# Hybrid conv/mLSTM layer: the first value projection by feature tiles between the modulation rows, in a written order; output-weight splits one step later; two up-projection slots loaded early

## The chip, the cores and the metric

One core of one Trainium2 chip. The metric is device microseconds of one execution, the median of the runs. TensorE (PE) does the matmuls, VectorE (DVE), ScalarE (ACT) and GpSimd (POOL) the elementwise work, SyncE (SP) issues the transfers.

## The reference, cut to what matters

A layer over 128 context and 2048 latent tokens, model width 1024, in float32. Each token's modulation comes from one of two conditioning vectors:

```python
mod = silu(c) @ w_mod + b_mod              # shift1, scale1, gate1, shift2, scale2, gate2
h = rmsnorm(x, norm1) * (1 + scale1) + shift1
z = h @ w_in                               # conv parts, q, k, v, o, gates
h_m, C, n, m = mlstm_bidir(q, k, v, gates, C0, n0, m0)
x = x + gate1 * (concat([y_sc, h_m]) @ w_out)
h2 = rmsnorm(x, norm2) * (1 + scale2) + shift2
up = conv3(h2 @ w_up);  a, gg = split(up)
x = x + gate2 * ((silu(gg) * a) @ w_down)
```

## The kernel before

The 2176 tokens are 17 chunks of 128, in blocks of three chunks (384 tokens; block 5 has 256). Features lie on the partitions, in eight tiles of 128. A float32 operand is split into a rounded high and a low part (`wh`, `wl` for weights, `hH`, `hL` for activations), and a product is three matmuls: high by high, high by low, low by high.

The **start stage** has four parts. `mod_pe` (L617 to L622) computes one row of 128 modulation values: it loads 512 KB of `w_mod` into one of five `wm` buffers, runs eight matmuls into an accumulator bank and adds the bias on DVE into `modT`. `mods` calls it for the scale and the shift row of a feature tile, and `affine` (L138) makes the factor `ab` of that tile. Sixteen such rows are computed on PE, and the rest later on DVE by `mod_dve` (L663 to L665). `squares` (L180 to L184) sums the squares of a block of x, ACT squaring and DVE adding; `inv_rms` (L147 to L151) turns the sum into a root on PE, DVE and POOL; `apply` first spreads that root over the partitions (`spread`, L158), then makes the eight tiles of `hH` and `hL` (L196 to L206). Even tiles go DVE L196, ACT L200, DVE L201; odd tiles go DVE L196, ACT L204, ACT L205, POOL L206. `vg` (L389 to L396) is the value and gate projection: for each chunk and each half of the columns an accumulator takes 24 matmuls of 264 columns over all eight tiles, ACT copies the values out (`row`), DVE adds the gate bias. `vg` runs for block 3, with `prep(4)` (squares, root and `apply` of block 4) between its groups, for block 4 with `prep(5)`, then for block 5; `heads` (L224 to L226, with the copy out at L404) follows with k, q and o, and beside it runs `side`: `first_stats` (squares of blocks 0 to 2), `mod_dve` and `down_sums`.

`out_proj` (L547 to L610) is 48 steps of 24 matmuls into one accumulator. In each step DVE adds the result to the row of x (L600), which frees the accumulator, and ACT and DVE gather the squares (L566, L572). Weights come in pairs, two steps of each four load them and the other two split them; from step 21 on DVE makes `wl` (L130) in front of that step's L600.

In the first **up stage** a slot of seven needs a block `F`, written by `sums` to DRAM (`tD`) and read back (L304), and split on ACT (L314) and DVE (L315). `split` does both at one place.

The framework's scheduler sets each engine's order from priorities, except where `in_order` ties the instructions of each engine to the order of the program.

Of the kernel before, what the change touches and what calls it, by code (L numbers as in the profile page):

```python
# [42 lines left out]
def bc(ap, shape):  # L43
    return ap.to_broadcast(shape)
# [13 lines left out]
def hymba_kernel(ctx: ExitStack, tc: tile.TileContext, I, O):  # L58
# [63 lines left out]
    def load_w(src, n=1024):  # L122
        return split_w(get_w(src, n), n)

    def split_w(st, n=1024, whole=False):
        wh = wp.tile([P, WN], F32R, name="wh")
        S.activation(wh[:, :n], st[:, :n], AF.Copy)  # L127
        wl = wp.tile([P, WN], F32R, name="wl")
        if whole:
            V.tensor_sub(wl[:, :n], st[:, :n], wh[:, :n].bitcast(F32))  # L130
            return wh, wl
        for a in (0, n // 2):
            G.tensor_sub(wl[:, a:a + n // 2], st[:, a:a + n // 2], wh[:, a:a + n // 2].bitcast(F32))  # L133
        return wh, wl
# [35 lines left out]
    def rcol(b):  # L170
        t0, n = BL[b]
        return rc[:, t0 // P:(t0 + n) // P]
# [11 lines left out]
            V.tensor_add(ss[:, :n], ss[:, :n], sq[:, :n])  # L184
        return ss

    def apply(b, xt, norm):
        t0, n = BL[b]
        rb = spread(rcol(b), n)
        hH, hL = h_pair()  # L190
        sh = 0 if norm == 0 else 24
        for k in range(KT):
            x = xt[k // 4][:, k % 4]
            for a, e, v in spans(t0, t0 + n):
                a, e = a - t0, e - t0
                V.scalar_tensor_tensor(x[:, a:e], x[:, a:e], ab[:, norm, k, v:v + 1], rb[:, a:e],  # L196
                                       op0=ALU.mult, op1=ALU.mult)
                sv = modT[:, sh + k, v:v + 1]
                if k % 2 == 0:
                    S.activation(hH[:, k, a:e], x[:, a:e], AF.Identity, bias=sv)  # L200
                    V.scalar_tensor_tensor(hL[:, k, a:e], x[:, a:e], sv, hH[:, k, a:e].bitcast(F32),  # L201
                                           op0=ALU.add, op1=ALU.subtract)
                else:
                    S.activation(x[:, a:e], x[:, a:e], AF.Identity, bias=sv)  # L204
                    S.activation(hH[:, k, a:e], x[:, a:e], AF.Copy)  # L205
                    G.tensor_sub(hL[:, k, a:e], x[:, a:e], hH[:, k, a:e].bitcast(F32))  # L206
        return hH, hL
# [146 lines left out]
    with ExitStack() as ph1:  # L354
# [21 lines left out]
        def load_vg(j):  # L376
            return [load_w(I["w_vg"][j, kk], WN) for kk in range(2)]

        def vg(blocks, hs, ws):
            for b in blocks:  # L380
                hH, hL = hs[b]
                for j in range(2):
                    for c in chunks(b):
                        o = c * P - BL[b][0]
                        acc = acc_tile()
                        for k in range(KT):
                            w_h, w_l = (x[:, (k % 4) * 264:(k % 4 + 1) * 264] for x in ws[2 * j + k // 4])
                            a_h, a_l = hH[:, k, o:o + P], hL[:, k, o:o + P]
                            PE.matmul(acc[:, :264], a_h, w_h, start=(k == 0), stop=False)  # L389
                            PE.matmul(acc[:, :264], a_h, w_l, start=False, stop=False)  # L390
                            PE.matmul(acc[:, :264], a_l, w_h, start=False, stop=(k == KT - 1))
                        r = rp.tile([P, 384], F32, name="row")[:, :258].rearrange("p (h d) -> p h d", h=2)
                        G.memset(r[:, :, 128:129], 1.0)
                        S.activation(r[:, :, :P], acc[:, :256].rearrange("p (h d) -> p h d", h=2), AF.Copy)
                        Q.dma_start(vD[c][:, 2 * j:2 * j + 2], r)
                        V.tensor_add(gates[:, c, j * 8:(j + 1) * 8], acc[:, 256:264],  # L396
                                     bgate[:, j * 8:(j + 1) * 8])
                        yield

        def head(w, b, h, hs, dst, func, scale):  # L400
# [144 lines left out]
        def out_proj(grps, defer, ws, hook):  # L545
# [25 lines left out]
                if m:  # L571
                    V.tensor_add(sss[b][:, :n], sss[b][:, :n], sq[:, :n])  # L572

            rows, got, behind, squared, held, sss = [], [], [], [], [], {}
            for k in range(2):
                load_r(k)
            yield
            for k, (g, m, b) in enumerate(steps):
                grp, (t0, n) = grps[g], BL[b]
                hook()  # L580
                load_r(k + 2)
                while squared:
                    add(*squared.pop())
                if len(behind) > 1:
                    squared.append(close(*behind.pop(0)))
                if k + 4 < len(steps):
                    if k % 4 < 2:
                        got.append(get_w(I["w_out"][steps[k - k % 4 + 4 + k % 4][1]]))
                    else:
                        ws.append(split_w(got.pop(0), whole=k > 20))  # L590
                w, xr = ws[m % 2], rows.pop(0)
                acc = gemm(w, early[b], n)
                if k % 4 == 3:
                    del ws[:2]
                if held and k == held[0] + 4:
                    stats(held[1], [sss[b] for b in held[1]])
                    held = []
                for a, e, v in spans(t0, t0 + n):
# [13 lines left out]

        hs = {}
        with tc.tile_pool(name="start", bufs=1, side="right") as stp:
            def mod_pe(mt):
                st = stp.tile([P, 1024], F32, name="wm", bufs=5)
                Q.dma_start(st, I["w_mod"][mt])  # L617
                ps = acc_tile()
                for k in range(KT):
                    PE.matmul(ps[:, :P], st[:, k * P:(k + 1) * P], bc(csil[:, k, None, :], [P, 64, 2]),  # L620
                              start=(k == 0), stop=(k == KT - 1))
                V.tensor_scalar(modT[:, mt, :], ps[:, :2], bmod[:, mt:mt + 1], None, op0=ALU.add)  # L622

            def mods(k0, k1):
                for k in range(k0, k1):
                    mod_pe(8 + k)
                    mod_pe(k)
                    affine(0, k, k + 1)

            Q.dma_start(bmod, I["b_mod"])  # L630
            mod_pe(8)
            Q.dma_start(nrm, I["norms"])
            mod_pe(0)
            affine(0, 0, 1)
            Q.dma_start(ident, I["ident"])
            mods(1, 2)
            xs = {3: load_x(3, I["x"], xp, "xt", 2)}
            ss = squares(3, xs[3])
            mods(2, 4)
            ws = load_vg(0)  # L640
            inv_rms(ss, 384, rcol(3))
            mods(4, 8)
            hs[3] = apply(3, xs[3], 0)
            ws += load_vg(1)
            Q.dma_start(bgate, I["b_gate"].to_broadcast([P, 16]))
            cB = stp.tile([P, 2, 1024], F32, name="cB")

            def late():
# [18 lines left out]
                        affine(1, 0, KT)  # L667
                    yield

            def prep(b):  # L670
                xs[b] = load_x(b, I["x"], stp, "xs", 4)
                ss = squares(b, xs[b])
                yield
                inv_rms(ss, BL[b][1], rcol(b))
                yield
                hs[b] = apply(b, xs[b], 0)
                yield
# [42 lines left out]
            late()  # L720
            mod = mod_dve()
            side = chain(first_stats(mod), mod, down_sums())
            run(vg((3,), hs, ws), prep(4))
            run(vg((4,), hs, ws), prep(5))
            run(vg((5,), hs, ws))
            run(heads(BB, hs, 16, kD, AF.Copy, 1.0), side)
            run(heads(BB, hs, 12, qD, AF.Copy, QS), side)
# [392 lines left out]
        until(46, sums(0, fpool, (1,), (6, 0)))  # L1120
        prods = stages(st)
        ahead = [next(prods) for _ in range(2)]
        run(fill)
        in_order(first)

# [22 lines left out]
    with ph2:  # L1148
# [31 lines left out]
            V.tensor_mul(t2[:, 0, :n], t2[:, 0, :n], t2[:, 1, :n])  # L1180
            Q.dma_start(uD[j][:, hf * n:(hf + 1) * n], t2[:, 0, :n])

        split(0, ORDER[2])
        side = sums(1, fpool)
        cv = iter(())
        while ahead:
# [16 lines left out]
            if hf and j == FT - 1 and i == 0:  # L1203
                first_forms()
            if not hf and j == 0 and i + 3 < 7:
                split(0, ORDER[i + 3])
            kind = "ababaca"[i]
            for p in range(npair):
                if i in (0, 1, 5):
# [269 lines left out]
```

## Time and profile before

| | us |
|---|---|
| median of 3 runs | 2503.4 (2498.62 to 2506.39) |
| the profiled execution | 2510.81 |
| its span, first to last instruction | 2509.0 |
| PE busy | 2457.2 |
| DVE busy | 1637.3 |
| ACT busy | 1126.0 |
| POOL busy | 523.7 |

A row of the timeline gives the start in the span, the duration, engine, line and operation, and in brackets the idle time of that engine just before it with what ended it. PEclk is the granted TensorE clock, 1.00 being 2.4 GHz and 0.50 being 1.2 GHz.

### The profile page before, as it was taken

To read this page: it belongs to the slowest core of one execution; us is meant where nothing else is said; L and a number is where in the kernel's file an instruction comes from. 1 tells how busy PE (TensorE), PEld (TensorE's weight loads), DVE (VectorE), ACT (ScalarE), POOL (GpSimd) and SP (SyncE) were. 2 spreads that over 40 slices of the span, in tenths; PEclk is the share of its full clock that TensorE was granted. 3 is DMA by queue.
4 is the path that set the end of the run, shared out by engine and by line. 5 is a ranking of instruction groups with operands and counts; after the bars stand their busy time and mean duration, and the time that the engine had idled before them with its cause. 6 is when DMAs were issued, how large, how long until landed. Compare 5 with 4: busy or idle time off the path is not lost.

```text
span 2509.0 us, 42463 instructions
## 1 busy us (share of the span) xinstructions
PE 2457.2 (98%) x16127; PEld 2355.5 (94%) x16127; DVE 1637.3 (65%) x2670; ACT 1126.0 (45%) x2062; POOL 523.7 (21%) x468
## 2 busy tenths in 40 slices
PE   7999999999999999999999999999999999999998
PEld 7999999999999999989999999788888899999998
DVE  3994552332465676687678667876777786787586
ACT  3521153233545564364455445554555553444342
POOL 2442233121344450012112111022112200000000
PEclk9999999999999999999999999999999999999999
DMA  7873773365767887754125222522222286866674
GB/s 271 269 238 128 278 249 126 101 196 172 243 200 233 280 262 241 247 206 148 67 83 184 84 83 92 169 93 95 89 85 88 87 257 200 260 205 215 185 231 128
DMA packets 280766, 443.41 MB, mean 177 GB/s; under 512 B 23266, under 2 KB 206194, under 8 KB 278898
## 3 DMA queue, kind: packets, MB, share of 16 engines
q1 hardware_dynamic: 280562, 440.70, 53.8%
q8 instruction: 127, 2.08, 0.3%
q14 instruction: 77, 0.63, 0.1%
HBM read 334.72 MB, written 105.89 MB: 176 GB/s over the span
## 4 chain that ended last, share of the span: by engine, by line
PE 82%; DVE 7%; DMA 6%; ACT 2%; issue 2%; POOL 1%; SPq 0%; DVEq 0%; ACTq 0%; POOLq 0%
PE acc L224 9%; PE acc L226 9%; PE acc L225 9%; PE pa L1216 6%; PE pa L1218 6%; PE pa L1217 6%; PE d L1371 5%; PE d L1372 5%; PE d L1370 5%; PE pb L1216 3%; PE pb L1218 3%; PE pb L1217 3%; PE pc L1216 2%; PE pc L1217 2%; PE pc L1218 2%
## 5 line engine op out<-in xcount | busy, mean ns | idle before, releaser
L224 PE MATMUL acc<-hH,wh 128*128 128x384 f32 (+1 forms) x1536 | 511.9, 333 | 7.3 <-DVE row L600 5.5
L226 PE MATMUL acc<-hH,wl 128*128 128x384 f32 (+1 forms) x1536 | 504.9, 329 | 0.0
L225 PE MATMUL acc<-hL,wh 128*128 128x384 f32 (+1 forms) x1536 | 504.4, 328 | 0.0
L1370 PE MATMUL d<-bh,wh 128*128 128x272 f32 x1232 | 356.4, 290 | 0.7 <-ACT raw L1228 0.7
L1372 PE MATMUL d<-bh,wl 128*128 128x272 f32 x1232 | 356.8, 290 | 0.0
L1371 PE MATMUL d<-bl,wh 128*128 128x272 f32 x1232 | 356.1, 289 | 0.0
L1216 PE MATMUL pa<-tH,wh 128*128 128x288 f32 (+1 forms) x1056 | 348.1, 330 | 5.4 <-ACT tH L314 2.2
L1218 PE MATMUL pa<-tH,wl 128*128 128x288 f32 (+1 forms) x1056 | 347.5, 329 | 1.6 <-DVE wl L333 1.6
L1217 PE MATMUL pa<-tL,wh 128*128 128x288 f32 (+1 forms) x1056 | 347.8, 329 | 1.1 <-DVE tL L315 1.1
L333 POOL TENSOR_TENSOR wl<-st,wh 128x512 fp32r<-128x512 f32 x123 | 170.2, 1384 | 706.0 <-ACT wh L332 704.7
L224 PEld LDWEIGHTS acc<-hH,wh 128*128 128x128 f32 x1536 | 290.6, 189 | 8.8 <-issue 6.8
L133 POOL TENSOR_TENSOR wl<-wst,wh 128x512 fp32r<-128x512 f32 (+1 forms) x136 | 200.1, 1493 | 451.2 <-ACT wh L127 393.6
L225 PEld LDWEIGHTS acc<-hL,wh 128*128 128x128 f32 x1536 | 290.7, 189 | 0.3 <-issue 0.2
L226 PEld LDWEIGHTS acc<-hH,wl 128*128 128x128 f32 x1536 | 290.3, 189 | 0.2 <-issue 0.2
L1159 DVE SCALAR_TENSOR_TENSOR tt<-raw,fw,tt 128x127 f32<-128x127 f32 (+4 forms) x264 | 244.1, 945 | 1.4 <-ACT tt L1165 0.3
L1370 PEld LDWEIGHTS d<-bh,wh 128*128 128x128 f32 x1232 | 232.7, 189 | 1.3 <-ACT raw L1228 1.1
L1371 PEld LDWEIGHTS d<-bl,wh 128*128 128x128 f32 x1232 | 232.6, 189 | 0.2
L1372 PEld LDWEIGHTS d<-bh,wl 128*128 128x128 f32 x1232 | 232.5, 189 | 0.0
L1216 PEld LDWEIGHTS pa<-tH,wh 128*128 128x128 f32 x1056 | 198.9, 188 | 22.2 <-ACT wh L332 4.1
L1218 PEld LDWEIGHTS pa<-tH,wl 128*128 128x128 f32 x1056 | 199.7, 189 | 17.6 <-DVE wl L333 2.0
L1217 PEld LDWEIGHTS pa<-tL,wh 128*128 128x128 f32 x1056 | 199.3, 189 | 17.2 <-DVE tL L315 1.5
L332 ACT ACTIVATE wh<-s 128x512 fp32r<-128x512 f32 x176 | 110.8, 629 | 179.2 <-PE pc L1217 92.5
(250 smaller groups left out, 4829.3 us busy)
## 6 DMA issues: line engine op xcount, KB each, us to landing
st<-in_w_up SPq DMA_DIRECT2D x88, 512.0 KB, 4.5
us<-uD SPq DMA_DIRECT2D x48, 544.0 KB, 5.0
wst<-in_w_in SPq DMA_DIRECT2D x48, 512.0 KB, 3.7
uD<-tt SPq DMA_DIRECT2D x44, 544.0 KB, 2.7
R<-nD SPq DMA_DIRECT2D x34, 512.0 KB, 4.3
wm<-in_w_modr SPq DMA_DIRECT2D x32, 512.0 KB, 5.5
wst<-in_w_out SPq DMA_DIRECT2D x24, 512.0 KB, 5.0
st<-wsD SPq DMA_DIRECT2D x32, 384.0 KB, 3.1
```

Of the source, the lines that this page charges most:

```text
L133: G.tensor_sub(wl[:, a:a + n // 2], st[:, a:a + n // 2], wh[:, a:a + n // 2].bitcast(F32))
L224: PE.matmul(acc[:, :n], w_h, hH[:, k, :n], start=(k == 0), stop=False)
L225: PE.matmul(acc[:, :n], w_h, hL[:, k, :n], start=False, stop=False)
L226: PE.matmul(acc[:, :n], w_l, hH[:, k, :n], start=False, stop=(k == KT - 1))
L333: (G if on_pool else V).tensor_sub(wl, a, wh.bitcast(F32))
L1159: V.scalar_tensor_tensor(o, i, w, o, op0=ALU.mult, op1=ALU.add)
L1216: PE.matmul(acc, wh[:, w], rh, start=(kk == 0 and i in (0, 1, 5)), stop=False, skip_group_check=True)
L1217: PE.matmul(acc, wh[:, w], rl, start=False, stop=False, skip_group_check=True)
L1218: PE.matmul(acc, wl[:, w], rh, start=False, stop=(kk == 3), skip_group_check=True)
L1370: PE.matmul(acc, wh[:, c], uh, start=(kk == 0), stop=False)
L1371: PE.matmul(acc, wh[:, c], ul, start=False, stop=False)
L1372: PE.matmul(acc, wl[:, c], uh, start=False, stop=(kk == KH - 1))
```

## The change

**Start.** The two modulation rows of a feature tile share one `S` bank, of which there is one. The loads of x for block 3 are issued ahead of the third modulation row. The value projection of block 3 is done by feature tile: `vg_first(k)` adds tile k to all six groups (four accumulators and the two halves of `y`), eighteen matmuls, between the modulation rows or behind them. ACT copies the spread root of block 3 out of PSUM (`rb`); `norm` applies one or two tiles at a time. The squares, root and `norm` of block 4 and the squares of block 5 stand inside this sequence, and the six copies out (`vg_out`) behind the squares of block 5. `in_order(0)` ties the order of all engines up to there. `prep` is left for block 5 alone.

**Output projection.** From step 21 on the DVE subtraction that makes `wl` is put off to the next step, behind that step's add and close (`trail`). From step 24 on both loads of a pair are issued in the first step of four.

**Up stage.** The first two `F` loads (`get_f`) are issued before the last of the fill is run, and the split (`put_f`) stays where it was.

```diff
-    def split_w(st, n=1024, whole=False):
+    def split_w(st, n=1024, trail=None):
...
-        if whole:
-            V.tensor_sub(wl[:, :n], st[:, :n], wh[:, :n].bitcast(F32))
+        if trail is not None:
+            trail.append(lambda: V.tensor_sub(wl[:, :n], st[:, :n], wh[:, :n].bitcast(F32)))
...
-                if k + 4 < len(steps):
-                    if k % 4 < 2:
-                        got.append(get_w(I["w_out"][steps[k - k % 4 + 4 + k % 4][1]]))
-                    else:
-                        ws.append(split_w(got.pop(0), whole=k > 20))
+                while trail:
+                    trail.pop()()
+                if k - k % 4 + 4 < len(steps):
+                    if k % 4 < (2 if k < 24 else 1):
+                        got.extend(get_w(I["w_out"][steps[k + 4 + i][1]]) for i in range(1 if k < 24 else 2))
+                    elif k % 4 > 1:
+                        ws.append(split_w(got.pop(0), trail=trail if k > 20 else None))
...
+            def vg_first(k):
...
+                for i in range(6):
+                    j, c = divmod(i, 3)
+                    w_h, w_l = (x[:, (k % 4) * 264:(k % 4 + 1) * 264] for x in ws[2 * j + k // 4])
+                    a_h, a_l = hH[:, k, c * P:(c + 1) * P], hL[:, k, c * P:(c + 1) * P]
+                    PE.matmul(vacc[i][:, :264], a_h, w_h, start=(k == 0), stop=False)
...
+            xs = {3: load_x(3, I["x"], xp, "xt", 2)}
+            get_m(9, 1, 10)
+            raw = get_vg(0)
+            mods(0, 1)
...
+            mods(7, 8)
+            ws[1], ws[3] = (split_w(w, WN) for w in raw)
+            norm(3, rb, 6, 7)
+            vg_first(3)
+            rb4 = spread(rcol(4), 384)
+            norm(4, rb4, 0, 1)
+            vg_first(4)
+            norm(4, rb4, 2, 3)
             Q.dma_start(bgate, I["b_gate"].to_broadcast([P, 16]))
+            vg_first(5)
+            norm(4, rb4, 4, 5)
+            vg_first(6)
+            norm(4, rb4, 6, 7)
+            vg_first(7)
+            ss = squares(5, xs[5])
+            for i in range(6):
+                vg_out(BL[3][0] // P + i % 3, i // 3, vacc[i])
+            in_order(0)
...
-            run(vg((3,), hs, ws), prep(4))
-            run(vg((4,), hs, ws), prep(5))
+            run(vg((4,), hs, ws), prep(5, ss))
...
+        got_f = [get_f(0, i) for i in ORDER[2:4]]
         run(fill)
```

On ACT at the end of the value projection of block 3, the order before, with buffer numbers (`xs_474` and `xs_476` hold block 4, `xs_721` and `xs_723` block 5; `row<-acc` is a copy out of an accumulator of block 3):

```order
L183 ACTIVATE sq_492<-xs_476 128x384
L394 ACTIVATE row_626<-acc_601 128x2x128
L183 ACTIVATE sq_495<-xs_476 128x384
L183 ACTIVATE sq_498<-xs_476 128x384
L180 ACTIVATE ss_725<-xs_721 128x256
L183 ACTIVATE sq_727<-xs_721 128x256
L183 ACTIVATE sq_730<-xs_721 128x256
```

And now, from the last tiles of `norm(4)` on (without buffer numbers; the 256-wide `xs` is block 5, `xt` block 0):

```order
L200 ACTIVATE hH<-xs,modT 128x384
L204 ACTIVATE xs<-xs,modT 128x384
L205 ACTIVATE hH<-xs 128x384
L180 ACTIVATE ss<-xs 128x256
L183 ACTIVATE sq<-xs 128x256 x2
L180 ACTIVATE ss<-xt 128x384
L183 ACTIVATE sq<-xs 128x256 x5
L382 ACTIVATE row<-acc 128x2x128 x4
L382 ACTIVATE row<-y 128x2x128
```

The copies out stood between the squares, one after each finished group; now the first of them stands behind all of `norm(4)` and all squares of block 5.

On PE at the same place, after the change, with buffer numbers (`y_346` is the last accumulator of block 3, `acc_711` the first of block 4, `ss_651` the sum of squares of block 5):

```order
L654 MATMUL y_346<-wh_516,hH_294 128x264
L655 MATMUL y_346<-wl_518,hH_294 128x264
L656 MATMUL y_346<-wh_516,hL_295 128x264
L147 MATMUL st_771<-ones_79,ss_651 128x1 x2
L397 MATMUL acc_711<-wh_256,hH_296 128x264
L398 MATMUL acc_711<-wl_258,hH_296 128x264
```

The root of block 5 (L147) stands between the last matmul of block 3 and the first of block 4.

On DVE in the output projection, at the split for step 44, before:

```order
L288 TENSOR_TENSOR tL<-F,tH 128x288 x2
L572 TENSOR_TENSOR ss<-ss,sq 128x256
L130 TENSOR_TENSOR wl<-wst,wh 128x1024
L600 SCALAR_TENSOR_TENSOR row<-acc,modT,row 128x256
L270 TENSOR_TENSOR F<-F,rb 128x1152
L572 TENSOR_TENSOR ss<-ss,sq 128x384
```

And now (L600 has become L605, L572 has become L575):

```order
L288 TENSOR_TENSOR tL<-F,tH 128x288 x2
L575 TENSOR_TENSOR ss<-ss,sq 128x256
L605 SCALAR_TENSOR_TENSOR row<-acc,modT,row 128x256
L270 TENSOR_TENSOR F<-F,rb 128x1152
L575 TENSOR_TENSOR ss<-ss,sq 128x384
L130 TENSOR_TENSOR wl<-wst,wh 128x1024
```

The row that makes `wl` has moved behind the add that frees the accumulator, and with it behind a 1152-wide multiply and a sum of squares.

## Rows read from the trace of the kernel before

**Rows 1.** The page: busy time of TensorE over the whole span with its share and instruction count, and the shares of the chain that ended last.
```profile
PE 2457.2 (98%) x16127; PEld 2355.5 (94%) x16127; DVE 1637.3 (65%) x2670; ACT 1126.0 (45%) x2062; POOL 523.7 (21%) x468
PE 82%; DVE 7%; DMA 6%; ACT 2%; issue 2%; POOL 1%; SPq 0%; DVEq 0%; ACTq 0%; POOLq 0%
```

**Rows 2.** Timeline of TensorE in the start stage, the rows with the long idle times: start, duration, engine, line, operation, then idle time before it and what ended it.
```profile
6.62 8.83 PE L620 MATMUL acc<-csil,wm 128*128 128x128 f32 x64 [6.62 <-DMA wm<-in_w_mod]
16.32 7.38 PE L620 MATMUL acc<-csil,wm 128*128 128x128 f32 x64 [0.87 <-DMA wm<-in_w_mod]
...
25.91 0.93 PE L158 MATMUL st<-ident,rc 128*128 128x128 f32 x6 [1.64 <-POOL rc L151]
26.68 16.08 PE L620 MATMUL acc<-csil,wm 128*128 128x128 f32 x128
...
46.24 0.39 PE L389 MATMUL acc<-wh,hH 128*128 128x264 f32 x1 [0.96 <-ACT hH L205]
...
48.77 0.39 PE L391 MATMUL acc<-wh,hL 128*128 128x264 f32 x1 [2.02 <-POOL hL L206]
...
61.16 0.83 PE L147 MATMUL st<-ones,ss 128*128 128x1 f32 x6 [1.26 <-DVE ss L184]
...
63.30 0.93 PE L158 MATMUL st<-ident,rc 128*128 128x128 f32 x6 [0.72 <-POOL row L393]
```

**Rows 3.** Windows view, core 0: stretch and its length, busy time of PE, PEld, DVE, ACT and POOL (instructions), granted TensorE clock, DMA share and GB/s.
```profile
10.00:20.00 10.00, 9.13 (x82) 8.97 (x82) 4.87 (x13) 3.97 (x8) 0.00 (x0) 1.00 1.04 403
26.70:30.10 3.40, 3.40 (x19) 3.40 (x18) 2.72 (x5) 2.54 (x5) 2.10 (x3) 0.50 0.37 147
64.30:67.70 3.40, 3.40 (x18) 3.40 (x17) 3.40 (x7) 2.84 (x6) 0.50 (x1) 0.50 0.76 204
989.20:992.60 3.40, 3.29 (x10) 3.32 (x11) 3.33 (x9) 2.51 (x6) 0.00 (x0) 0.51 0.57 204
1051.00:1054.40 3.40, 3.23 (x19) 3.27 (x20) 1.75 (x3) 2.08 (x4) 0.37 (x1) 1.00 0.84 306
```

**Rows 4.** Timeline of TensorE inside one value-projection group of block 3: start and duration of two matmuls with one between them.
```profile
49.84 0.28 PE L390 MATMUL acc<-wl,hH 128*128 128x264 f32 x1
...
50.09 0.28 PE L389 MATMUL acc<-wh,hH 128*128 128x264 f32 x1
```

**Rows 5.** Timelines of ScalarE and VectorE, 49 to 73 us: the steps that make the normalised tiles of block 4, the squares of block 5, one copy out, and the activation of the conditioning rows.
```profile
49.48 1.91 ACT L654 ACTIVATE cB<-cB 128x2048 f32<-128x2048 f32 x1
60.72 1.31 ACT L183 ACTIVATE sq<-xs 128x256 f32<-128x256 f32 x3
64.81 0.39 ACT L394 ACTIVATE row<-acc 128x256 f32<-128x256 f32 x1 [1.29 <-PE acc L391]
65.09 0.61 ACT L200 ACTIVATE hH<-xs,modT 128x384 fp32r<-128x384 f32 x1
65.60 0.61 ACT L204 ACTIVATE xs<-xs,modT 128x384 f32<-128x384 f32 x1
66.61 0.51 ACT L205 ACTIVATE hH<-xs 128x384 fp32r<-128x384 f32 x1
...
66.39 0.60 DVE L196 SCALAR_TENSOR_TENSOR xs<-xs,ab,st 128x384 f32<-128x384 f32 x1
66.91 0.61 DVE L201 SCALAR_TENSOR_TENSOR hL<-xs,modT,hH 128x384 fp32r<-128x384 f32 x1
```

**Rows 6.** Timelines around 141 us: the last long modulation reduction on VectorE before the add, a square on ScalarE that waits for VectorE, the copies out behind it, and TensorE's first matmul after its idle time.
```profile
130.90 1.23 DVE L663 SCALAR_TENSOR_TENSOR y<-wm,cB 128x1024 f32<-128x1024 f32 x1
132.70 0.53 ACT L183 ACTIVATE sq<-xt 128x384 f32<-128x384 f32 x1 [11.62 <-DVE ss L184]
140.78 0.85 ACT L404 ACTIVATE row<-acc 128x384 f32<-128x384 f32 x2
...
141.30 0.44 PE L224 MATMUL acc<-hH,wh 128*128 128x384 f32 x1 [1.76 <-ACT row L404]
```

**Rows 7.** Timelines of TensorE, VectorE and ScalarE in the output projection: TensorE's three waits for L600, and the `wl` splits before them.
```profile
989.31 0.66 PE L224 MATMUL acc<-hH,wh 128*128 128x384 f32 x1 [2.23 <-DVE row L600]
1051.17 0.41 PE L224 MATMUL acc<-hH,wh 128*128 128x384 f32 x1 [1.78 <-DVE row L600]
1057.12 0.42 PE L224 MATMUL acc<-hH,wh 128*128 128x384 f32 x1 [1.52 <-DVE row L600]
...
987.41 1.23 DVE L130 TENSOR_TENSOR wl<-wst,wh 128x1024 fp32r<-128x1024 f32 x1 [2.21 <-ACT wh L127]
1049.40 1.23 DVE L130 TENSOR_TENSOR wl<-wst,wh 128x1024 fp32r<-128x1024 f32 x1 [1.35 <-ACT wh L127]
...
1048.30 1.06 ACT L127 ACTIVATE wh<-wst 128x1024 fp32r<-128x1024 f32 x1 [1.91 <-DMA wst<-in_w_out]
```

**Rows 8.** The first up slots: the queue of SyncE, ScalarE's first split, and two of TensorE's waits for it.
```profile
1070.57 0.32 SPq L304 DMA_DIRECT2D F<-tD  x1
1070.99 0.85 SPq L560 DMA_DIRECT2D xD<-row  x2
...
1075.99 2.22 ACT L314 ACTIVATE tH<-F 128x1152 fp32r<-128x1152 f32 x2 [1.64 <-DMA F<-tD]
...
1077.20 0.40 PE L1216 MATMUL pa<-tH,wh 128*128 128x288 f32 x1 [1.55 <-ACT tH L314]
1084.20 0.40 PE L1216 MATMUL pb<-tH,wh 128*128 128x288 f32 x1 [0.57 <-ACT tH L314]
```

More of the change, by code (lines that the diff above doesn't have):

```diff
@@ L185, in squares, with apply @@
         return ss
-    def apply(b, xt, norm):
+    def apply(b, xt, norm, ks=range(KT), rb=None, pair=None):
         t0, n = BL[b]
-        rb = spread(rcol(b), n)
-        hH, hL = h_pair()
+        rb = spread(rcol(b), n) if rb is None else rb
+        hH, hL = pair or h_pair()
         sh = 0 if norm == 0 else 24
-        for k in range(KT):
+        for k in ks:
             x = xt[k // 4][:, k % 4]
@@ L377, in load_vg, with vg_out @@
             return [load_w(I["w_vg"][j, kk], WN) for kk in range(2)]
+        def vg_out(c, j, acc):
+            r = rp.tile([P, 384], F32, name="row")[:, :258].rearrange("p (h d) -> p h d", h=2)
+            G.memset(r[:, :, 128:129], 1.0)
+            S.activation(r[:, :, :P], acc[:, :256].rearrange("p (h d) -> p h d", h=2), AF.Copy)
+            Q.dma_start(vD[c][:, 2 * j:2 * j + 2], r)
+            V.tensor_add(gates[:, c, j * 8:(j + 1) * 8], acc[:, 256:264],
+                         bgate[:, j * 8:(j + 1) * 8])
         def vg(blocks, hs, ws):
@@ L391, in vg @@
                             PE.matmul(acc[:, :264], a_l, w_h, start=False, stop=(k == KT - 1))
[L392 to L397, printed above, removed]
+                        vg_out(c, j, acc)
                         yield
@@ L572, in add @@
                     V.tensor_add(sss[b][:, :n], sss[b][:, :n], sq[:, :n])
-            rows, got, behind, squared, held, sss = [], [], [], [], [], {}
+            rows, got, trail, behind, squared, held, sss = [], [], [], [], [], [], {}
             for k in range(2):
@@ L614, in hymba_kernel @@
         with tc.tile_pool(name="start", bufs=1, side="right") as stp:
[L615 to L622, printed above, removed]
+            wm = []
@@ L624, in mods, with get_m @@
+            def get_m(*mts):
+                for mt in mts:
+                    st = stp.tile([P, 1024], F32, name="wm", bufs=5)
+                    Q.dma_start(st, I["w_mod"][mt])
+                    wm.append(st)
             def mods(k0, k1):
                 for k in range(k0, k1):
-                    mod_pe(8 + k)
-                    mod_pe(k)
-                    affine(0, k, k + 1)
+                    ps = pm.tile([P, 512], F32, name="S")
+                    for i in range(2):
+                        st = wm.pop(0)
+                        for kk in range(KT):
+                            PE.matmul(ps[:, i * P:(i + 1) * P], st[:, kk * P:(kk + 1) * P],
+                                      bc(csil[:, kk, None, :], [P, 64, 2]), start=(kk == 0), stop=(kk == KT - 1))
+                    for i, mt in enumerate((8 + k, k)):
+                        V.tensor_scalar(modT[:, mt, :], ps[:, i * P:i * P + 2], bmod[:, mt:mt + 1], None, op0=ALU.add)
+                    affine(0, k, k + 1)
@@ new lines, in get_vg @@
+            def get_vg(kk):
+                return [get_w(I["w_vg"][j, kk], WN) for j in range(2)]
+            def vg_first(k):
+                if k == 0:
+                    y = pm.tile([P, 2, 512], F32, name="y")
+                    vacc.extend([acc_tile() for _ in range(4)] + [y[:, 0], y[:, 1]])
+                hH, hL = hs[3]
+                for i in range(6):
[3 more added lines that the diff above has]
+                    PE.matmul(vacc[i][:, :264], a_h, w_h, start=(k == 0), stop=False)
+                    PE.matmul(vacc[i][:, :264], a_h, w_l, start=False, stop=False)
+                    PE.matmul(vacc[i][:, :264], a_l, w_h, start=False, stop=(k == KT - 1))
@@ L630, in hymba_kernel @@
+            vacc, ws = [], [None] * 4
             Q.dma_start(bmod, I["b_mod"])
-            mod_pe(8)
+            get_m(8)
             Q.dma_start(nrm, I["norms"])
-            mod_pe(0)
-            affine(0, 0, 1)
+            get_m(0)
             Q.dma_start(ident, I["ident"])
+            xs = {3: load_x(3, I["x"], xp, "xt", 2)}
+            get_m(9, 1, 10)
+            raw = get_vg(0)
+            mods(0, 1)
+            ss = squares(3, xs[3])
+            get_m(2, 11)
             mods(1, 2)
-            xs = {3: load_x(3, I["x"], xp, "xt", 2)}
@@ L638, in hymba_kernel @@
-            ss = squares(3, xs[3])
-            mods(2, 4)
-            ws = load_vg(0)
+            get_m(3, 12)
+            mods(2, 3)
             inv_rms(ss, 384, rcol(3))
-            mods(4, 8)
-            hs[3] = apply(3, xs[3], 0)
-            ws += load_vg(1)
-            Q.dma_start(bgate, I["b_gate"].to_broadcast([P, 16]))
+            ws[0], ws[2] = (split_w(w, WN) for w in raw)
+            xs[4] = load_x(4, I["x"], stp, "xs", 4)
+            get_m(4, 13)
+            mods(3, 4)
@@ new lines, in hymba_kernel, with norm @@
+            hs[3], hs[4] = h_pair(), h_pair()
+            rb = stp.tile([P, 384], F32, name="rb")
+            S.activation(rb, spread(rcol(3), 384)[:, :384], AF.Copy)
+            def norm(b, rb, *ks):
+                apply(b, xs[b], 0, ks, rb, hs[b])
+            norm(3, rb, 0, 1)
+            raw = get_vg(1)
+            get_m(5, 14)
+            mods(4, 5)
+            norm(3, rb, 2, 3)
+            vg_first(0)
+            get_m(6, 15)
+            mods(5, 6)
+            norm(3, rb, 4)
@@ new lines, in hymba_kernel @@
+            vg_first(1)
+            get_m(7)
+            xs[5] = load_x(5, I["x"], stp, "xs", 4)
+            ss = squares(4, xs[4])
+            mods(6, 7)
+            norm(3, rb, 5)
+            vg_first(2)
+            inv_rms(ss, 384, rcol(4))
+            mods(7, 8)
[6 more added lines that the diff above has]
+            norm(4, rb4, 2, 3)
@@ L668, in mod_dve, with prep @@
                     yield
-            def prep(b):
-                xs[b] = load_x(b, I["x"], stp, "xs", 4)
-                ss = squares(b, xs[b])
+            def prep(b, ss):
                 yield
@@ L1181, in conv @@
             Q.dma_start(uD[j][:, hf * n:(hf + 1) * n], t2[:, 0, :n])
-        split(0, ORDER[2])
+        put_f(got_f.pop(0), 0, ORDER[2])
         side = sums(1, fpool)
@@ L1205, in hymba_kernel @@
             if not hf and j == 0 and i + 3 < 7:
-                split(0, ORDER[i + 3])
+                put_f(got_f.pop(0) if got_f else get_f(0, ORDER[i + 3]), 0, ORDER[i + 3])
             kind = "ababaca"[i]
```

## The prediction

> **What bounds the kernel now.** I read the page first. TensorE is busy for 2457.2 of the 2509.0 us of the span, and it is 82% of the chain that ended last [rows 1]. The change removes no matmul of TensorE: it splits the same groups in another order. What it can win or lose is therefore only TensorE's idle time, some 52 us in all, and the stretches at half clock. So I went next to the timeline of TensorE and listed each idle time with what ended it, for the three places that the diff touches: the start [rows 2], the output projection [rows 7] and the first up slots [rows 8]. In the start the listed waits make 6.62 + 0.87 + 1.64 + 0.96 + 2.02 + 1.26 + 0.72 = 14.1 us, with two small ones 14.6; the first 6.62, for the first load, are out of reach of any reordering. In the output projection there are three waits for L600, 2.23 + 1.78 + 1.52 = 5.5 us. At the first up slots the two waits shown are 1.55 and 0.57; with five like them they make 5.5 us. Third, the windows view for the clock: after idle times TensorE ran 3.4 us at 0.50 from 26.7 and from 64.3, 19 and 18 matmuls, where the full clock gives 82 x 3.4/9.13 = 31 in that time [rows 3], so each such stretch loses about 1.7 us. The most that all this could give is about 27 us: 8.0 and two windows (3.4) in the start, 5.5 and one window (1.7) in the output projection, 5.5 and two windows (3.4) at the slots.
>
> **The start.** The time to the end of the modulation rows first. A row costs (16.08 - 1.7)/8 = 1.8 us at full clock, since the stretch of 128 matmuls has one half-clock window in it [rows 2, 3]; the first row is cold, 3.5 us. A matmul of the value projection takes 0.12 us from start to start [rows 4], so a feature tile of eighteen takes 2.16. In the new order x of block 3, 1.57 MB, is loaded ahead of the third row. At the 403 GB/s that the queue moves then [rows 3] this is 3.9 us of delay at most and nothing at least, since the row is needed only at about 12 us. I take 1.5 us there, 0.3 for the single `S` bank (one DVE read of 0.2 before the next pair may start), and 1.7 in three later waits for loads: 3.4 us, bounds 0.9 (today's wait at 16.32) and 6.6 (x and the two 0.54 MB loads of the projection ahead of the rows). These replace today's 0.87 and 1.64. The waits at 46.24 and 48.77, for the split of the weights and the first tiles, go: these are ready while modulation rows run. Up to the spread of block 4, TensorE then needs 6.6 + 3.5 + 15 x 1.8 + 4 x 2.16 + 3.3 (two roots and spreads of 0.73 + 0.93) + 3.4 = 52.4 us.
>
> From there four tiles of the projection remain, 8.6 us, so TensorE is through at 61.0. The next instruction is the root of block 5, then the first group of block 4, which reuses the first accumulator of block 3. Both wait for what stands behind `norm(4)` and `squares(5)` on ACT and DVE, whose order is now tied. `norm(4)` is then a chain from engine to engine: for each pair of tiles ACT L200 0.61, DVE L201 0.61, DVE L196 0.60, ACT L204 0.61, ACT L205 0.51 [rows 5], each waiting for the one before: 2.94 us, four times, and 0.6 for the first L196: 12.4 us from 52.4, 64.8. The activation of the conditioning rows, 1.91 us on ACT [rows 5], stands just ahead; I add 0.6 for it, 65.4. The eight squares of block 5 come at 1.31/3 = 0.44 [rows 5], with the last DVE add 3.9 us: 69.3. TensorE stands idle from 61.0 to 69.3, **8.3 us**, and the first group of block 4 can start at 69.9, when the first copy out (0.39) and its gate bias are done. Bounds: if the chain ran at DVE's own rate, twelve instructions of 0.6, the tiles would be ready at 59.6 and the squares at 63.5, 2.5 us idle; with the whole activation and a slow chain it is 10 us. I take 8.3, since in the written order nothing can be put between the steps of a pair.
>
> Idle time to the heads is then 6.6 + 3.4 + 8.3 = 18.3, against 14.6: **+3.7 us**. Half-clock stretches: today two, 3.4 us lost; then one surely, behind the 8.3, and one as likely as not among the first rows, 2.6 lost: **-0.8**. The clock behind the long wait is read from the output projection: after 2.23 us of idle the granted clock was 0.51 from 989.2, after 1.78 us at 1051.17 it stayed 1.00 [rows 3, 7]. The Trainium skill's page "TensorE: Matmul & The Clock Gate" (Part 1) says that the slow clock is the default and that activity releases it, so that a rest of TensorE costs speed afterwards; by that rule the new wait costs 10.0 us and not 8.3, and without it the whole sum would be 1.7 lower. The two rows agree with it in direction.
>
> The same page ("Engine queue depths") says that ScalarE and VectorE take their queues strictly in order, a rule that speaks against this change: a copy out whose accumulator has long been ready does not pass the squares. The trace agrees: at 140.78 two copies left ACT together, behind squares that had waited for DVE (11.62 us once), and TensorE had stood 1.76 us for the first [rows 6].
>
> That wait at 141 is the next place. DVE now has thirty rather than 23 of the long modulation reductions in front of the add on which these squares wait, 7 x 1.23 = 9 us more [rows 6], but starts on them about as much earlier. I take no change, bounds -1.8 (the wait goes) and +5 (half of the 9 us falls on TensorE).
>
> **The output projection.** Today the `wl` split waits 1.35 to 2.2 us for ACT on DVE's queue, takes 1.23, and L600, which frees the accumulator, stands behind it [rows 7]. Moved behind L600, the split no longer holds the accumulator, but it is late for the step that reads it: the high part came from ACT at 1049.36, after the load, so `wl` cannot end before 1050.6 where TensorE wants it at about 1049.8, and now a 1152-wide multiply and a sum of squares stand ahead of it. The wait of 1.78 stays nearly whole, as a wait for `wl`; of the 2.23 some 0.7 goes, and the 1.52 goes nearly whole. Loading both weights in the first step of four gives the second half a step. Sum **-2 us**; bounds -7.2 (all three waits and the half-clock stretch at 989) and +1 (each wait a little longer).
>
> **The up slots.** The first F load was issued at 1070.57 and waited for the data to land in DRAM; ACT split it at 1075.99 [rows 8]. Issued ahead of the stores it still waits for the same landing, so the wait of 1.55 us stays. The second load goes ahead of two stores, 0.85 us on SP's queue, but the split that it feeds stands behind another weight on ACT now, and the wait of 0.57 for it can grow to 1.9. **+1 us**, bounds -2 and +2.3.
>
> **Sum.** +3.7 - 0.8 + 0 - 2 + 1 = +1.9 us. The profiled execution took 2510.81, 7.4 above the median; the change of it is carried over to the median: 2503.4 + 1.9 = 2505.3, so 2505.
>
> **The rivals.** *Faster: the hole before block 4 does not open.* If ACT and DVE do `norm(4)` at DVE's rate, the wait is 2.5 us; idle time to the heads is 6.6 + 3.4 + 2.5 = 12.5, -2.1, with one window fewer -1.7; if then the output projection gives its 7.2 and the slots nothing, the time is 2492.4, and with 2 us of the slots 2490.4. For it: four waits of the start have their cause removed. Against it: the order of ACT and the durations of the chain. It decides from a wait below 3 us. *Slower: the add at 141 is late.* The hole makes the heads later, but DVE's seven more reductions come first; if the add is then done some 5 us after TensorE wants the accumulator, the copies behind it on ACT hold TensorE for 6.8 rather than 1.76: +5, and with the +1.9 and one more window of 1.7 the time is 2512; with the hole at 10 us it is 2514. It decides from an add that ends behind about 137 us. For it: ACT waited 11.62 us for this add already. Against: DVE begins its reductions earlier. *The output projection doesn't give anything*, because each wait for L600 becomes one for `wl`: 2507, inside the forecast.
>
> **How the numbers follow.** A measurement of this kernel can tell about 0.3%, 7.5 us, from no change: 2495.9 to 2510.9. The forecast, with the rival without gain in the output projection, 0.73; faster 0.14; slower 0.13. The forecast's own bounds, from the hole (2.5 to 10), the add (-1.8 to +5), the projection (-7.2 to +1) and the slots, not all at one end, are 2497 to 2511; the range takes in the nearer half of both rivals: 2494 to 2513.
>
> **What would show it.** In the profile after: a wait of TensorE of about 8 us near 61, ended by DVE's sum of squares, followed by a stretch at 0.5; the first head matmul some 3 us later than before; no waits at the weight split of block 3; a wait near 141 of 0 to 4 us; waits for `wl` in place of those for L600. The forecast is wrong if the wait near 61 is below 3 us, or if the one at 141 is above 5.

## The result, and the profile after

| | us, median (runs) | ratio to before, 95% interval |
|---|---|---|
| before | 2503.14 (2494.60 to 2506.46, 19) | |
| changed | 2508.11 (2504.66 to 2513.56, 19) | 1.0028 [1.0019, 1.0036] |

The changed kernel is slower: by 5.0 us between the medians, by 7 by the ratio. That lies inside the range and, just, inside 0.3%. Its profiled execution took 2509.99 (span 2508.2), near its own median, while the one of before, 2510.81, was 7.7 us above its median. A difference of these two traces is therefore read place by place, not from their ends.

The page after, busy time and chain, against [rows 1]:

```profile
PE 2453.2 (98%) x16127; PEld 2351.2 (94%) x16127; DVE 1633.8 (65%) x2670; ACT 1126.1 (45%) x2063; POOL 525.5 (21%) x468
PE 83%; DVE 8%; DMA 5%; ACT 2%; issue 2%; POOL 1%; SPq 0%; DVEq 0%; ACTq 0%; POOLq 0%
```

The totals hardly differ; an argument from shares ends here. The timeline of TensorE after in the start stage, against [rows 2]:

```profile
5.39 5.53 PE L635 MATMUL S<-csil,wm 128*128 128x128 f32 x32 [5.39 <-DMA wm<-in_w_mod]
13.70 3.81 PE L635 MATMUL S<-csil,wm 128*128 128x128 f32 x32 [2.78 <-DMA wm<-in_w_mod]
17.99 4.14 PE L635 MATMUL S<-csil,wm 128*128 128x128 f32 x32 [0.48 <-PE S L635]
...
30.75 2.05 PE L635 MATMUL S<-csil,wm 128*128 128x128 f32 x16 [1.82 <-DMA wm<-in_w_mod]
...
74.86 0.98 PE L147 MATMUL st<-ones,ss 128*128 128x1 f32 x4 [12.42 <-DVE gates L384]
...
143.22 0.44 PE L224 MATMUL acc<-hH,wh 128*128 128x384 f32 x1 [1.05 <-ACT row L407]
```

The waits for the first tiles behind the weight split (46 and 49 us before) are gone. In their place is one wait of 12.42 us. The windows view after around it (columns as in rows 3):

```profile
53.70:62.40 8.70, 8.70 (x72) 8.53 (x70) 5.40 (x9) 5.61 (x8) 3.29 (x3) 1.00 0.86 294
62.40:74.90 12.50, 0.08 (x2) 0.07 (x1) 7.55 (x16) 8.63 (x21) 3.18 (x9) 0.68 0.52 211
74.90:80.70 5.80, 5.80 (x27) 5.80 (x28) 4.37 (x12) 3.24 (x9) 1.19 (x7) 0.50 0.72 212
```

TensorE works without a gap up to 62.4, stands for 12.4 us, and then works 5.8 us at 0.50 (1.2 GHz), which costs up to 2.9 more. What it waited for stands in the timelines of ScalarE and VectorE after:

```profile
54.32 1.90 ACT L728 ACTIVATE cB<-cB 128x2048 f32<-128x2048 f32 x1
57.19 0.60 ACT L200 ACTIVATE hH<-xs,modT 128x384 fp32r<-128x384 f32 x1
59.35 0.62 ACT L204 ACTIVATE xs<-xs,modT 128x384 f32<-128x384 f32 x1 [1.56 <-DVE xs L196]
60.00 0.53 ACT L205 ACTIVATE hH<-xs 128x384 fp32r<-128x384 f32 x1
60.43 0.60 ACT L200 ACTIVATE hH<-xs,modT 128x384 fp32r<-128x384 f32 x1
...
70.09 0.40 ACT L180 ACTIVATE ss<-xs 128x256 f32<-128x256 f32 x1
...
74.01 1.19 ACT L382 ACTIVATE row<-acc 128x256 f32<-128x256 f32 x4
...
52.02 1.74 DVE L196 SCALAR_TENSOR_TENSOR xt<-xt,ab,rb 128x384 f32<-128x384 f32 x1
55.82 0.60 DVE L196 SCALAR_TENSOR_TENSOR xs<-xs,ab,st 128x384 f32<-128x384 f32 x1
57.82 0.97 DVE L201 SCALAR_TENSOR_TENSOR hL<-xs,modT,hH 128x384 fp32r<-128x384 f32 x1 [1.40 <-ACT hH L200]
58.71 1.13 DVE L196 SCALAR_TENSOR_TENSOR xs<-xs,ab,st 128x384 f32<-128x384 f32 x2
...
70.83 3.88 DVE L184 TENSOR_TENSOR ss<-ss,sq 128x256 f32<-128x256 f32 x7 [1.85 <-ACT sq L183]
74.63 0.23 DVE L384 TENSOR_TENSOR gates<-acc,bgate 128x8 f32<-128x8 f32 x2
```

Read the brackets as a ball going to and fro: ACT idles 1.56 us for a DVE step, DVE idles 1.40 for an ACT step, and a pair of tiles takes 3.24 us (57.19 to 60.43). Four pairs, then the squares from 70.09, then the first copies out at 74.01, for accumulators that had all been finished by 62.4, and on VectorE the first gate bias (L384, to 74.86) behind the sum of squares (to 74.71).

In the output projection, the waits view of TensorE after, 970 to 1110 us (us in total, times, longest):

```profile
PE acc L226 <- DVE wl L130: 2.1, 5, 0.8
```

Against the 5.5 us of [rows 7] stand 2.1 us in five waits for `wl`, and no half-clock stretch up to 1066 us. One follows in the up slots (0.50 from 1084.2), where before had two.

### The profile page after: what moved, and what is told of

Its sections match the earlier page's. It is cut to its first block, busy times and chain, and to the rows that moved or that the text cites. A ratio compares the mean times of both kernels' runs of the same rounds, so it can differ in the third digit from the quotient of the medians.

```text
span 2508.2 us, 42462 instructions
## 1 busy us (share of the span) xinstructions
PE 2453.2 (98%) x16127; PEld 2351.2 (94%) x16127; DVE 1633.8 (65%) x2670; ACT 1126.1 (45%) x2063; POOL 525.5 (21%) x468
## 4 chain that ended last, share of the span: by engine, by line
PE 83%; DVE 8%; DMA 5%; ACT 2%; issue 2%; POOL 1%; SPq 0%; DVEq 0%; ACTq 0%; POOLq 0%
PE acc L226 9%; PE acc L224 8%; PE acc L225 8%; PE pa L1290 6%; PE pa L1288 6%; PE pa L1289 6%; PE d L1443 5%; PE d L1444 5%; PE d L1442 5%; PE pb L1288 3%; PE pb L1289 3%; PE pb L1290 3%; PE pc L1288 2%; PE pc L1289 2%; PE pc L1290 2%
```

## The experiments

Two theories. **A**: the start costs the time, by the order behind `norm(4)`; the output projection gives some back; the early loads do nothing. **B**: the start is about even, and the loss sits at the first up slots. First each part of the diff alone on the kernel before.

**start_only**: all of the diff in the start, nothing else. 

> The kernel before with the new start alone. Theory A (the start costs what the trace of after shows by the time of 900 matmuls, and the rest gives little): 5 us slower than before, 2507 to 2510, with TensorE idle for some 12 us near 62. Rival B (the start is about even, and the 5 us come from the first up slots or the output projection): within 2 us of before.

**out_only**: `split_w` and `out_proj` alone. 

> The kernel before with the output projection's change alone (split a step later, both loads in the first step of four). Theory A: 1 to 4 us faster than before, the three waits for L600 replaced by waits for wl of 2 us together. Rival B: 0 to 3 us slower, since each wait for L600 becomes a wait for wl of the same length.

**slots_only**: the `get_f`/`put_f` lines alone. 

> The kernel before with the two F loads issued early and nothing else. Theory A: within 2 us of before, the first split still waits for the landing in DRAM of what sums wrote. Rival B: 3 us or more slower, because the weight split ahead of the second slot's split on ScalarE stops TensorE longer and costs half-clock stretches.

**no_start**: the last two together. 

> The changed kernel with the old start: output projection and early F loads together. If the parts add up, 0.9977 x 1.0006 = 0.9983 of before, about 4 us faster; if the early loads take away what the output projection's change gives at the first up slots, no faster than before.

| | median us | before beside it | ratio |
|---|---|---|---|
| start_only | 2512.14 | 2502.94 | 1.0033 [1.0022, 1.0045] |
| out_only | 2496.88 | 2502.94 | 0.9977 [0.9967, 0.9986] |
| slots_only | 2504.29 | 2502.94 | 1.0006 [0.9996, 1.0017] |
| no_start | 2498.55 | 2502.31 | 0.9983 [0.9973, 0.9993] |

So the start costs 8.3 us (5.5 to 11.3), the output projection gives 5.8 (3.5 to 8.3), the early loads cost 1.5, which is not clear of zero. Both sizes are above what was expected (5, and 1 to 4). The last two add up. With the start the product is 1.0016, below the 1.0028 of the whole, by about what the three intervals allow. B is out.

In the waits view of out_only, 970 to 1110 us, and the first up matmul that had waited 1.55 us in [rows 8]:

```profile
PE acc L226 <- DVE wl L130: 2.5, 5, 0.8
...
1067.09 0.40 PE L1218 MATMUL pa<-tH,wh 128*128 128x288 f32 x1 [0.20 <-ACT tH L314]
```

The projection's own waits fell by 3 us, and the wait at the first up slot from 1.55 to 0.20. The granted clock is 1.00 from 970 to 1113, where the trace of before has three stretches near 0.5 (from 989.2, 1078 and 1095); as that execution was 7.7 us above its median, not all three need be usual. The work of `sums` that fills this slot is on the same DVE queue (L270 to L288 in the order shown with the change), so a split that no longer blocks the queue brings it forward too. That this is the cause of the second gain is read from the order and the two traces; no run separates it, nor the later split from the earlier loads, which out_only has together.

In slots_only the second slot's wait grew, as its price in the prediction said, from the 0.57 of [rows 8]:

```profile
1083.80 0.40 PE L1217 MATMUL pb<-tH,wh 128*128 128x288 f32 x1 [1.26 <-ACT tH L314]
```

Then the wait of 12.4 us, taken apart. All of these start from the changed kernel.

**copies_first**: the copies out ahead of the squares.

```diff
-            ss = squares(5, xs[5])
             for i in range(6):
                 vg_out(BL[3][0] // P + i % 3, i // 3, vacc[i])
+            ss = squares(5, xs[5])
             in_order(0)
```

> The changed kernel with the six copies out of block 3 ahead of the squares of block 5. If the wait of 12.4 us near 62 is the copies standing behind those squares, it shrinks by the 4 us that the squares take, to about 8.5, and the kernel is 4 us faster than the changed one, about 2504. If the wait were only the root of block 5 standing in TensorE's order, moving the copies leaves the wait near 62 at 12 us and the time at 2508.

**chain_open**: `apply` gets a `part`, 1 for the first step (L196) and 2 for the others.

```diff
-            norm(4, rb4, 0, 1)
+            apply(4, xs[4], 0, range(KT), rb4, hs[4], 1)
             vg_first(4)
-            norm(4, rb4, 2, 3)
+            apply(4, xs[4], 0, range(KT), rb4, hs[4], 2)
...
-            norm(4, rb4, 4, 5)
...
-            norm(4, rb4, 6, 7)
```

> The changed kernel with all eight first steps of norm(4) on VectorE ahead of its other steps, so that a pair no longer waits for the one before; the copies out stay behind the squares of block 5. If the chain between ACT and DVE sets the wait, norm(4) ends near 63.5 instead of 70.2 and the wait of 12.4 us near 62 shrinks to about 6: 2501 to 2502. If ACT's own work sets it, or POOL's share in the tiles, the wait stays above 10 us and the time near 2507.

**silu_last**: `in_order(0)` moved behind `late()`, so that the activation of the conditioning rows stands behind the copies out. 

> The changed kernel with the activation of the conditioning rows tied behind the copies out, no longer inside norm(3) and norm(4). If it delays the chain by its whole 1.9 us, the wait near 62 is 10.5 and the kernel 2 us faster than the changed one, 2506, as far as the modulation reductions, which need it, do not then come late for the squares near 141; if it was hidden, 2508 or, by those reductions, more.

**both_fixes**: copies_first and chain_open. 

> The changed kernel with both: the eight first steps of norm(4) first, and the copies out ahead of the squares of block 5. Theory: the wait near 62 falls to 1 to 3 us and the half-clock stretch behind it to one or none; 2494 to 2498. If the lost time only moves on (to the root of block 5 or to the reductions near 141), 2500 to 2503.

| | median us | before beside it | ratio | wait near 62 |
|---|---|---|---|---|
| copies_first | 2501.93 | 2502.94 | 0.9998 [0.9989, 1.0007] | 8.28 |
| chain_open | 2500.40 | 2500.85 | 1.0003 [0.9987, 1.0018] | 5.96 |
| silu_last | 2509.75 | 2500.85 | 1.0034 [1.0022, 1.0046] | 12.23 |
| both_fixes | 2494.06 | 2500.85 | 0.9967 [0.9954, 0.9980] | 1.65 |

The first matmul after the wait in copies_first, chain_open and both_fixes, from the timelines of TensorE:

```profile
71.15 0.59 PE L397 MATMUL acc<-wh,hH 128*128 128x264 f32 x1 [8.28 <-DVE gates L384]
```
```profile
68.29 0.98 PE L147 MATMUL st<-ones,ss 128*128 128x1 f32 x4 [5.96 <-DVE gates L387]
```
```profile
63.65 0.39 PE L400 MATMUL acc<-wh,hH 128*128 128x264 f32 x1 [1.65 <-DVE gates L387]
```

12.42 minus 4.14 for the squares, minus 6.46 for the chain: 1.82 is left if both are taken, and 1.65 is what both_fixes shows. The two causes add up to the wait but for this rest. With the squares later, the root of block 5 (L147) also left its place ahead of block 4's first matmul, as the rows with L397 and L400 show; in both_fixes it comes at 73, with waits of 0.40 and 0.69 at it and behind it. In time copies_first gained 7.5 us on the changed kernel by the two ratios, some 4 to 11 by their intervals, where 4 were expected; its first head matmul is 3.0 us earlier (104.62 for 107.62), and the rest of the gain is not explained. The third, the activation (1.90 at 54.32 in the timeline after), was mostly hidden. In silu_last the tiles of block 4 begin at 56.41 instead of 57.19, and ScalarE, without the activation, waits for VectorE instead:

```profile
55.33 0.62 ACT L204 ACTIVATE xt<-xt,modT 128x384 f32<-128x384 f32 x1 [1.51 <-DVE xt L196]
56.41 0.60 ACT L200 ACTIVATE hH<-xs,modT 128x384 fp32r<-128x384 f32 x1
...
55.22 0.60 DVE L196 SCALAR_TENSOR_TENSOR xs<-xs,ab,st 128x384 f32<-128x384 f32 x1
```

Of these 0.78 us, 0.60 is only that everything is earlier in this trace (the first L196 on `xs` at 55.22 instead of 55.82); 0.2 is gained, as the wait shows (12.23 for 12.42).

The copies out at 141 and 148 us then made TensorE wait 2.6 us in all, where after has 1.05; the expectation of 2 us was a miss.

**fixes_no_slots**: both_fixes with the F loads at their old place. 

> The same as both_fixes with the two F loads left where they were in the kernel before. Theory from slots_only (1.0006, interval 0.9996 to 1.0017): 0 to 3 us faster than both_fixes; rival: equal, the loads do not matter once the output projection runs without its waits.

**start_fixed**: start_only with both fixes. 

> The kernel before with the new start and both fixes of it (eight first steps of norm(4) first, copies out ahead of the squares of block 5), without the output projection's change and without the early F loads. Theory: what the new start lost was the wait near 62 alone, so that with it closed the start gains what was meant: 2 to 6 us faster than before. Rival: the new start is no better than the old one even so, because of the loads among the first rows, and the gain of both_fixes is the output projection's: within 2 us of before.

**x_later**: fixes_no_slots with the loads in another order.

```diff
+            get_m(9, 1)
             xs = {3: load_x(3, I["x"], xp, "xt", 2)}
-            get_m(9, 1, 10)
+            get_m(10)
```

> fixes_no_slots with x of block 3 loaded behind the third and fourth modulation rows instead of ahead of them. If the wait of 2 to 3 us near 13 is the load of x ahead of the third row, it goes, and with it the half-clock stretch near 15: 2 to 4 us faster than fixes_no_slots, 2489 to 2491. If the wait only moves to the squares or the next row's load, 2492 to 2494.

**no_pool_tiles**: fixes_no_slots with this line for block 4 on VectorE.

```diff
-                    G.tensor_sub(hL[:, k, a:e], x[:, a:e], hH[:, k, a:e].bitcast(F32))
+                    (V if part == 2 else G).tensor_sub(hL[:, k, a:e], x[:, a:e], hH[:, k, a:e].bitcast(F32))
```

> fixes_no_slots with the low part of the odd tiles of block 4 and block 5 made on VectorE instead of GpSimd where the two-part order is used (block 4). If a VectorE step that reads two tiles from SBUF is slowed by GpSimd working beside it, the four L204 of block 4 take 0.61 us instead of 0.95; if they are slow for another reason, they stay at 0.95. Time: VectorE has four more steps of 0.5 us and gives back 1.4, so within 2 us of fixes_no_slots, 2491 to 2495.

| | median us | before beside it | ratio |
|---|---|---|---|
| fixes_no_slots | 2492.99 | 2500.85 | 0.9958 [0.9946, 0.9971] |
| start_fixed | 2496.03 | 2502.31 | 0.9974 [0.9960, 0.9987] |
| x_later | 2492.30 | 2502.31 | 0.9955 [0.9942, 0.9968] |
| no_pool_tiles | 2494.27 | 2500.91 | 0.9971 [0.9960, 0.9983] |

start_fixed settles that what the new start lost lay in what the two fixes change: 1.0033 with the long wait, 0.9974 without (its wait there is 1.66). fixes_no_slots beats both kernels, by 10.5 us the one before; its distance from both_fixes is inside the intervals. x_later moved the wait at the third row and won nothing that can be told. The timelines of TensorE, of fixes_no_slots and then of x_later:

```profile
13.96 5.44 PE L638 MATMUL S<-csil,wm 128*128 128x128 f32 x32 [3.30 <-DMA wm<-in_w_mod]
```
```profile
12.17 3.81 PE L638 MATMUL S<-csil,wm 128*128 128x128 f32 x32 [0.48 <-PE S L638]
18.49 3.81 PE L638 MATMUL S<-csil,wm 128*128 128x128 f32 x32 [2.51 <-DVE ab L138]
```

The load no longer holds the second pair, which runs at full clock (3.81 us for 5.44); the third pair now waits for `ab`, since x comes later, and with it the sum of squares that is tied ahead of `ab` on VectorE.

no_pool_tiles is about VectorE's step L201 (L204 here). Groups by line and form on VectorE, from 50 us on, of after, and then of no_pool_tiles:

```profile
L196 DVE SCALAR_TENSOR_TENSOR xs<-xs,ab,st 128x384 f32<-128x384 f32 x8 | 4.6, 601 | 0.0
L201 DVE SCALAR_TENSOR_TENSOR hL<-xs,modT,hH 128x384 fp32r<-128x384 f32 x4 | 3.8, 957 | 5.1 <-ACT hH L200 5.1
L196 DVE SCALAR_TENSOR_TENSOR xt<-xt,ab,rb 128x384 f32<-128x384 f32 x2 | 2.3, 1174 | 0.0
```
```profile
L204 DVE SCALAR_TENSOR_TENSOR hL<-xs,modT,hH 128x384 fp32r<-128x384 f32 x4 | 2.4, 610 | 0.0
```

Beside GpSimd's tiles L201 takes 957 ns, without them 610. The time of the kernel did not gain by it: VectorE got back 4 x 0.35 us but took over four subtractions of 0.55 ahead of the gate bias, and the wait near 62 was 1.85 for 1.65.

## Why the prediction was right, point by point

**The class and the range were right, two terms of the sum were not**, and they lay on opposite sides: the start at +2.9 (+3.7 idle, -0.8 clock) measured 8.3, the output projection at -2 measured -5.8, the slots at +1 measured 1.5. The sum of the terms was +1.9, the change was 5.0 to 7. That the total came out within the range is in part luck: the start was missed by 5.4 us and the projection by 3.8 the other way.

*The wait before block 4.* The place and the order that makes it were as forecast; copies_first and chain_open show both halves of the cause. As releaser the forecast named the sum of squares, the row names the gate bias just behind it (74.71 and 74.86). The size was not as forecast: 12.4 for 8.3. The chain began at 55.82 (first L196 on `xs`), not at 52.4: two tiles of block 3 stood ahead on VectorE, the first L196 of them at 1.74 us while GpSimd split weights. That is 3.4. The chain then took 14.3 us up to the first square instead of 13.0: 1.3, most of it in the pairs, 3.24 each for 2.94, as L201 took 0.94 to 0.97 beside GpSimd where [rows 5] have 0.61. From the first square to TensorE it was 4.8 for 3.9: 0.9. TensorE itself came 1.4 later. 3.4 + 1.3 + 0.9 - 1.4 = 4.2. The error was to take the shortest row of each step, without asking what GpSimd does at that moment, and to start the chain as if VectorE were free. The trace of before had the longer row too, beside a step of GpSimd:

```profile
70.42 0.96 DVE L201 SCALAR_TENSOR_TENSOR hL<-xs,modT,hH 128x384 fp32r<-128x384 f32 x1 [1.32 <-ACT hH L200]
...
69.96 1.01 POOL L206 TENSOR_TENSOR hL<-xs,hH 128x384 fp32r<-128x384 f32 x1 [1.56 <-ACT hH L205]
```

*The other waits of the start.* 2.78 + 0.48 + 1.82 = 5.1 for my 3.4, inside the bounds. Idle time to the heads: 5.4 + 5.1 + 12.4 = 22.9 for 18.3.

*The clock.* One stretch, behind the long wait, as forecast, 5.8 us of work at half speed instead of 3.4. The early stretch that I gave an even chance did not come in the profile of the changed kernel; it did in that of fixes_no_slots (5.44 above). The price of 1.7 for a stretch of 3.4 us is half of its length; the counts beside it (19 and 18 matmuls for 31) give 1.3 to 1.4.

*The wait at 141* was 1.05, and TensorE ran at full clock behind it, where before it had waited 1.76 and then run a half-clock stretch. I took no change; the two traces show a gain of some 2 us. But the way to it was not as forecast. The add did come late, past the 137 us by which the slower rival was to be told. VectorE, before and after, and the first head matmul, before and after:

```profile
132.12 0.55 DVE L184 TENSOR_TENSOR ss<-ss,sq 128x384 f32<-128x384 f32 x1
...
100.15 0.34 PE L224 MATMUL acc<-hH,wh 128*128 128x384 f32 x1
```
```profile
140.24 0.55 DVE L184 TENSOR_TENSOR ss<-ss,sq 128x384 f32<-128x384 f32 x1
...
107.62 0.34 PE L224 MATMUL acc<-hH,wh 128*128 128x384 f32 x1
```

The add is 8.1 us later: seven more reductions stand in front of it, and VectorE began them at 77.59 instead of 77.81, not some 9 us earlier as the prediction had it. TensorE did not pay for it, because its heads began 7.5 us later and not 3. That this term held was luck: the larger hole hid the late add. The kernel came out slower by the hole, which was in the sum, made larger.

*The output projection.* The wait for L600 did become a wait for `wl`, as said, but of 0.2 to 0.8 each, not "nearly whole". The multiply and the sum of squares do stand in full between the add and the split (1051.77 to 1053.60). The step that failed kept the time at which ScalarE has the high part ready. Timelines of ScalarE, VectorE and TensorE after, at the place of the old wait of 1.78:

```profile
1050.15 1.05 ACT L127 ACTIVATE wh<-wst 128x1024 fp32r<-128x1024 f32 x1
...
1051.77 1.36 DVE L270 TENSOR_TENSOR F<-F,rb 128x1152 f32<-128x1152 f32 x1
1053.05 0.55 DVE L575 TENSOR_TENSOR ss<-ss,sq 128x384 f32<-128x384 f32 x1
1053.52 1.22 DVE L130 TENSOR_TENSOR wl<-wst,wh 128x1024 fp32r<-128x1024 f32 x1
...
1053.92 0.34 PE L224 MATMUL acc<-hH,wh 128*128 128x384 f32 x1
1054.79 0.45 PE L226 MATMUL acc<-hH,wl 128*128 128x384 f32 x1 [0.36 <-DVE wl L130]
```

Before, the high part came at 1049.36, just when TensorE could have begun the step (1051.17 - 1.78 = 1049.39). After, it comes at 1051.20, 2.7 us ahead of the step at 1053.92, no longer behind a wait for its load; so the multiply, the sum and most of the split pass while TensorE still works. The sum also left out that the same VectorE queue feeds the first up slot, if the reading above is right.

*The rival "the hole does not open"* was given 2492.4 with all of the projection's gain. In both_fixes, where the hole is closed by hand to 1.65, the time is 2494.06, beside 2500.85 for before.

## What to carry to other kernels

When an order is tied across engines, look for steps that hand a tile back and forth between two of them: their latencies add, and work that is ready on a third engine waits behind them. What frees a buffer for the bound engine (a copy out of an accumulator) belongs ahead of everything that engine does not need yet. And a queue that is unblocked can pay twice, once for who waited and once for the work behind; here the second gain is read from the order and not separated by a run.

## What the runs showed of the hardware

In these runs a VectorE step that reads two tiles from SBUF is slower while GpSimd works; one that reads a tile from SBUF and one from PSUM is not. For L201, which reads two from SBUF, no_pool_tiles shows it: 0.96 beside GpSimd, 0.61 without. For L196 it is read from the traces alone. With `rb` in SBUF it took 1.74 us (52.02, above) beside this row of GpSimd, from the timeline after:

```profile
49.51 5.45 POOL L133 TENSOR_TENSOR wl<-wst,wh 128x528 fp32r<-128x528 f32 x4
```

With the root in PSUM eight of them (L197 there) keep their pace, 4.28/8 = 0.54 from start to start, across two steps of GpSimd, from the timelines of fixes_no_slots:

```profile
55.30 4.28 DVE L197 SCALAR_TENSOR_TENSOR xs<-xs,ab,st 128x384 f32<-128x384 f32 x8
```
```profile
56.84 1.02 POOL L209 TENSOR_TENSOR hL<-xt,hH 128x384 fp32r<-128x384 f32 x1 [2.40 <-ACT hH L208]
58.41 1.03 POOL L209 TENSOR_TENSOR hL<-xs,hH 128x384 fp32r<-128x384 f32 x1 [0.55 <-ACT hH L208]
```

The Trainium skill's page "SBUF — State Buffer" ("SBUF: two separate sides") gives a reason: VectorE and GpSimd share one pair of ports, and the one that comes second waits for the whole instruction; for VectorE it names two SBUF inputs, against a step of GpSimd that reads SBUF, as a case. The trace agrees in kind: in the changed kernel L201 at 57.82 overlaps the step of GpSimd below by 0.56 us and took 0.35 longer than alone. That it waits for the whole of the other instruction is not shown.

```profile
57.36 1.02 POOL L206 TENSOR_TENSOR hL<-xt,hH 128x384 fp32r<-128x384 f32 x1 [2.40 <-ACT hH L205]
```

The copy `rb` into SBUF, which the change adds, thus made at least one of the steps that it serves slower.
